# Chores tied behind evictions in the retention, another product order in the convolution, and a reordered passage from projection to gate/up

## The chip, the cores and the metric

One Trainium2 chip, one of its cores. The metric is the device time of one execution in microseconds (us), the median of three runs. The engines are named as in the profile: PE is TensorE, DVE is VectorE, ACT is ScalarE, POOL is GpSimd, SP is SyncE, which here only issues DMA. Each engine runs its own list of instructions in order; the lists are fixed when the program is built.

## The reference

```python
mod = silu(c) @ ada_w + ada_b                      # shift, scale, gate for both sub-layers
h = x * (1 + scale_m) + shift_m                    # x: 2048 rows of 1024
z = h @ w_in                                       # 3 x 512 columns: conv, 4 x 512: retention q, k, v, g
y_conv = bg * causal_conv3(cg * xin, conv_w)
q, k = rotary(q), rotary(k) * 128 ** -0.5          # 4 heads of 128, chunks of 128 rows
r = head_groupnorm(((q k^T) * decay_mask) v + decayed_state(q, k, v))
mix = concat(y_conv, silu(g) * r) @ w_out
x = layernorm(2 ** 0.25 * x + gate_m * mix)
h = x * (1 + scale_f) + shift_f
x = layernorm(2 ** 0.25 * x + gate_f * ((silu(h @ w_gate) * (h @ w_up)) @ w_down))
```

## The kernel before

All matrices are fp32 and are multiplied as pairs of fp16 numbers, a high and a low part: `mm3` issues three matmuls (high by high, L135; high by low, L136; low by high, L137) that add into one PSUM bank. The wide products after the retention go block by block with Strassen's and Winograd's scheme, in which seven products of blocks and of sums of blocks stand for eight. One such product is 12 matmuls of 128 rows by 512 columns for each quarter. PSUM has eight banks, four handed out in turn as `mm` (`bank`) and four as `ax` (`aux`); a bank is used again only after VectorE or ScalarE has read it ("eviction").

The program has these stages, which a scheduler merges: it takes the instructions in the order of the Python code, works out times for them with a model of its own, and writes each engine's list. `tc.issue_after(x)` adds the condition that what is issued under it comes after instruction `x` on the engine of `x`.

1. **Retention**, a loop over `t`, 16 tiles of 128 rows. `gemm_ret(t, u)` makes one of four 512-column groups of a tile (24 matmuls). Group `u == 0` is evicted by DVE (L705), `u` 1 and 2 by ACT (L709), `u == 3` by ACT with Silu (L711). `rotary(t)` (L734 to L736 on DVE, two sums on POOL) needs L709; `ret_scores` multiplies the scores by the decay mask on DVE (L767); `ret_y` (L793, L796 on PE) needs that product. Between the groups stand chores: `ret_h(p)` scales and shifts x by `modulate` (L296, eight instructions on ACT), makes the block sums on POOL, and `ret_hsplit(p)` splits them into fp16 pairs (L130 on ACT, L131 on DVE), which feed later tiles; `h_again` and `chores` do the same for tiles whose h planes go to DRAM (`hcscr`) for the convolution.
2. **Convolution**, `conv_pair(u, b)` for six column groups `u` and two row halves `b`. The products are numbered 0 to 6; `hp_load(b, m)` brings plane `m` of h from `hcscr`, `cw_split(u)` makes the weights (ACT L880 and L888, POOL sums, DVE L889).
3. **Output projection**, `op_half(t, half)`, evicted by DVE L1307 into the rows `y`; then `norm1` (statistics on DVE, L1278 on ACT), `y_store`, and `h2_pair(j)` with `h2_turn(j)`, which make and transpose the planes for the next stage (POOL L1342 to L1350, ACT L1351 and L1354, DVE L1341, L1352 and L1355, seven transposing DMAs L1374 on SP).
4. **Gate and up products**, `gu(q, bl)`, with weights from `gu_load`, `gu_scale`, `gu_split1` (planes A11, A12, S1, A22) and `gu_split2` (planes S2, S3, S4: L1421 to L1423, then ACT L1426 and DVE L1427).
5. **Down projection** and the second LayerNorm.

SP issues the loads in one list (`hcscr` and weight loads, transposes, stores of `y` and `u`), ACT issues the stores to `hcscr`.

## Time and profile before

| | us |
|---|---|
| median of three runs | 2106.2 |
| the three runs | 2104.92, 2106.2, 2108.79 |
| the profiled execution | 2106.87 |
| its span, first to last instruction | 2104.7 |

The span is 2.2 us shorter than the device time of the same execution. The mean clock granted to PE was 0.987 of full speed. Times below are counted from the span's start; line numbers are those of the kernel before.

### The profile page before, as it was taken

The page shows a single profiled execution, that of the slowest core. Times are in us where ns is not written, and L with a number is a line of the kernel's source. Part 1 is how long each engine was busy: PE and PEld are TensorE (multiplying, and loading weights), DVE is VectorE, ACT ScalarE, POOL GpSimd, SP SyncE. Part 2 cuts the span into 40 slices and gives each one's busy share as a digit, 9 for nine tenths or more (in the row PEclk, how much of TensorE's full clock was granted, in tenths as well). Part 3 has the DMA queues.
Part 4 walks back from the last instruction along what each step waited for, and adds up shares of the span by engine and source line. Part 5 has one row for each costly group of instructions (what it writes and reads, how often), then busy time and mean ns, then how long its engine had stood idle before and what let it go on. Part 6 is the DMA issues. An engine that isn't in the chain of part 4 may idle for free.

```text
span 2104.7 us, 24640 instructions
## 1 busy us (share of the span) xinstructions
PE 2023.1 (96%) x9631; PEld 948.0 (45%) x9631; DVE 1463.8 (70%) x1793; ACT 666.9 (32%) x728; POOL 904.9 (43%) x751
## 2 busy tenths in 40 slices
PE   8899998989899999789999999999999999999998
PEld 3354554444344544334444444444444444444443
DVE  7898846567686577766678768877777354478564
ACT  5523443433422223332323223343433222212210
POOL 3554855555642377742323114544444143134232
PEclk9999999999999999999999999999999999999999
DMA  9048544576873298742444553434343665375321
GB/s 380 26 135 260 163 133 110 161 236 212 269 307 125 85 251 195 186 128 71 149 170 166 184 189 126 160 126 154 131 150 120 237 263 198 139 272 190 150 77 74
DMA packets 189492, 361.06 MB, mean 172 GB/s; under 512 B 118080, under 2 KB 118080, under 8 KB 166592
## 3 DMA queue, kind: packets, MB, share of 16 engines
q1 hardware_dynamic: 181168, 344.55, 49.1%
q10 hardware_dynamic: 8208, 14.95, 2.1%
q8 instruction: 75, 1.23, 0.2%
q14 instruction: 41, 0.34, 0.0%
HBM read 231.26 MB, written 100.93 MB: 158 GB/s over the span
## 4 chain that ended last, share of the span: by engine, by line
PE 42%; DVE 8%; POOL 5%; DMA 5%; issue 2%; ACT 2%; SPq 0%; POOLq 0%; DVEq 0%; ACTq 0%
PE mm L135 7%; PE mm L136 7%; PE mm L137 7%; PE ax L135 7%; PE ax L137 7%; PE ax L136 7%; DMA pg<-yscr 2%; DMA pg<-in_w_dn_dram 2%; POOL pg L1342 1%; DVE pg L1617 1%; ACT pg L1278 1%; DVE wdm L87 1%; DVE pg L1618 1%; DVE pg L1482 1%; POOL rs L1270 1%
## 5 line engine op out<-in xcount | busy, mean ns | idle before, releaser
L135 PE MATMUL mm<-pg,pg 128*128 128x512 f16 x1604 | 609.4, 382 | 18.4 <-ACT pg L1426 8.2
L136 PE MATMUL mm<-pg,pg 128*128 128x512 f16 x1604 | 611.2, 381 | 0.0
L137 PE MATMUL mm<-pg,pg 128*128 128x512 f16 x1604 | 609.5, 381 | 1.7 <-DVE pg L889 1.7
L135 PE MATMUL ax<-pg,pg 128*128 128x512 f16 x1220 | 462.9, 380 | 9.3 <-DVE t2k L973 3.8
L137 PE MATMUL ax<-pg,pg 128*128 128x512 f16 x1220 | 462.6, 380 | 1.5 <-DVE pg L889 1.5
L136 PE MATMUL ax<-pg,pg 128*128 128x512 f16 x1220 | 463.3, 380 | 0.0
L136 PEld LDWEIGHTS <-pg 128*128 128x128 f16 x2888 | 283.3, 98 | 350.4 <-issue 23.7
L135 PEld LDWEIGHTS <-pg 128*128 128x128 f16 x2888 | 283.3, 98 | 345.7 <-issue 9.5
L137 PEld LDWEIGHTS <-pg 128*128 128x128 f16 x2888 | 283.1, 98 | 340.7 <-issue 6.4
L1476 POOL TENSOR_TENSOR pg<-pg,t2k 128x512 f32<-128x512 f32 x44 | 57.9, 1315 | 383.2 <-DVE t2k L1475 207.6
L131 DVE SCALAR_TENSOR_TENSOR pg<-pg,p2s,pg 128x2048 f16<-128x2048 f32 (+1 forms) x42 | 95.9, 2294 | 134.5 <-ACT pg L130 134.4
L130 ACT ACTIVATE pg<-pg,p2s 128x2048 f16<-128x2048 f32 (+1 forms) x42 | 77.6, 1858 | 262.2 <-PE mm L136 114.1
L87 DVE TENSOR_REDUCE m<-pg 128x2 bf16<-128x2048 f32 (+1 forms) x38 | 86.3, 2275 | 20.9 <-DMA pg<-in_w_gu_dram 10.8
L525 PE MATMUL mm<-pg,pg 128*128 128x512 f16 x384 | 89.1, 387 | 5.6 <-DVE pg L533 2.5
L1481 ACT ACTIVATE pg<-t2k,ivg 128x512 f32<-128x512 f32 x44 | 31.6, 717 | 178.1 <-DVE t2k L1480 178.1
L1530 DVE TENSOR_TENSOR pg<-pg,pg 128x2048 f16<-128x2048 f32 (+1 forms) x22 | 46.3, 2103 | 44.6 <-ACT pg L1529 44.6
L1413 DVE TENSOR_TENSOR pg<-pg,pg 128x2048 f16<-128x2048 f32 x22 | 51.7, 2349 | 31.7 <-ACT pg L1412 31.7
L1529 ACT ACTIVATE pg<-pg 128x2048 f16<-128x2048 f32 (+1 forms) x22 | 37.3, 1697 | 99.6 <-DMA wscr<-pg 57.8
L131 DVE SCALAR_TENSOR_TENSOR pg<-pg,hs,pg 128x1024 f16<-128x1024 f32 x32 | 49.4, 1547 | 26.8 <-ACT pg L130 26.6
L1270 POOL TENSOR_SCALAR rs<-mv 128x1 f32<-128x1 f32 x32 | 30.5, 957 | 82.2 <-DVE mv L1268 79.6
L1583 POOL TENSOR_TENSOR pg<-pg,pg 128x2048 f32<-128x2048 f32 (+1 forms) x6 | 26.9, 4491 | 82.0 <-DVE pg L131 38.6
L525 PEld LDWEIGHTS <-pg 128*128 128x128 f16 x384 | 37.5, 99 | 52.4 <-issue 7.7
(278 smaller groups left out, 2782.7 us busy)
## 6 DMA issues: line engine op xcount, KB each, us to landing
pg<-wscr SPq DMA_DIRECT2D x28, 1024.0 KB, 4.8
pg<-in_w_gu_dram SPq DMA_DIRECT2D x22, 1024.0 KB, 4.9
uscr<-pg SPq DMA_DIRECT2D x44, 512.0 KB, 2.8
pg<-in_w_dn_dram SPq DMA_DIRECT2D x22, 1024.0 KB, 5.9
pg<-in_adaT_dram SPq DMA_DIRECT2D x21, 1024.0 KB, 8.2
wscr<-pg SPq DMA_DIRECT2D x77, 256.0 KB, 2.9
yscr<-pg SPq DMA_DIRECT2D x16, 1024.0 KB, 4.3
pg<-uscr SPq DMA_DIRECT2D x16, 1024.0 KB, 5.7
```

What stands on the lines that cost most here:

```text
L87: return nc.vector.tensor_reduce(dst, src, axis=AX.X, op=OP.max, apply_absolute_value=True).ins
L130: nc.scalar.activation(hi, src, AF.Copy, scale=s)
L131: nc.vector.scalar_tensor_tensor(lo, src, s, hi, op0=OP.mult, op1=OP.subtract)
L135: nc.tensor.matmul(ps, l_hi, r_hi, start=start, stop=False, skip_group_check=again)
L136: nc.tensor.matmul(ps, l_hi, r_lo, start=False, stop=False, skip_group_check=again)
L137: return nc.tensor.matmul(ps, l_lo, r_hi, start=False, stop=stop, skip_group_check=again).ins
L525: nc.tensor.matmul(ps, hv[:, a, k, o], w[:, k], start=n == 0 and k == k0, stop=n == 2 and k == k1 - 1)
L1270: nc.gpsimd.tensor_scalar(rs, mv[:, 1:2], EPS / (ALPHA * ALPHA), None, op0=OP.add)
L1413: nc.vector.tensor_sub(wa[:, 2048:], pg, wa[:, :2048])
L1476: nc.gpsimd.tensor_add(e5, e5, p1)
L1529: nc.scalar.activation(o[:, :n, 0], src, AF.Copy)
L1530: nc.vector.tensor_sub(o[:, :n, 1], src, o[:, :n, 0])
```

## The change

- In the retention, `ret_h` and `ret_hsplit` come on ACT after the eviction of `gemm_ret(t, 2)`, and `h_again` and `chores` after that of `gemm_ret(t, 3)`. In the last tile the h planes 6 and 3 change places in the order of loading, and so does the list `ahead`.
- In `conv_pair` product 3, into a fresh bank, is issued before product 6, which adds into an old one.
- In the passage from stage 3 to stage 4 all of the last projections are issued before their LayerNorms; `gu_split2(0)` runs on VectorE, `gu_split2(1)` is done early; the scaling of the last two rows (`norm1`'s ACT instruction) comes after the products have begun; `h2_pair(3)` writes into the scratch page `s32[0]` and not in place; and `gu(0, 1)` and `gu(1, 1)` get `late=True`, by which the products with the planes S2, S4 and S3 come last.

```diff
+    evicted = [None]
...
-            nc.scalar.activation(dst, ps, AF.Copy, scale=iv)
+            evicted[0] = nc.scalar.activation(dst, ps, AF.Copy, scale=iv).ins
...
-            hp_load(0, 6)
+            hp_load(0, 3)
         if t % 2 == 0 and p < 8:
-            ret_h(p)
-            ret_hsplit(p)
+            with tc.issue_after(evicted[0]):
+                ret_h(p)
+                ret_hsplit(p)
...
+        with tc.issue_after(evicted[0]):
+            if t in AGAIN:
+                h_again(AGAIN.index(t))
+            elif chores:
+                chores.pop()()
...
         prod(pa, 1, False, True)
+        pd = new()
+        prod(pd, 3, True, True)
         prod(pb, 6, False, True)
         nc.vector.scalar_tensor_tensor(p1, pb, iv, p1, op0=OP.mult, op1=OP.add)
         nc.gpsimd.tensor_add(e5, e5, p1)
-        pd = new()
-        prod(pd, 3, True, True)
...
-        fp = yp[j] if tp else page()
+        fp = tp or page()
...
-        prod(pb, "S2", T2, True, True)
-        nc.vector.tensor_add(u2, pb, p1)
+        if not late:
+            prod(pb, "S2", T2, True, True)
+            nc.vector.tensor_add(u2, pb, p1)
...
+        if late:
+            prod(pb, "S2", T2, True, True)
+            nc.vector.tensor_add(u2, pb, p1)
+            prod(pc, "S4", B22, False, True)
+            nc.vector.tensor_add(u2, pc, u2)
         prod(pb, "S3", T3, False, True)
...
-            gu_split2(0, nc.gpsimd)
+            gu_split2(0, nc.vector)
+            for t in (2 * j, 2 * j + 1):
+                op_half(t, 1)
+            free(*wo_pages[2:])
+            for n in range(2):
+                gu_pages[n].append(page(F16, at=-1))
+            gu_split2(1, nc.vector)
...
-    gu_split1(1)
-    gu_split2(1, nc.vector)
+    gu(0, 1, late=True)
+    with tc.issue_after(gu_act[0]):
+        gu_split1(1)
+    with tc.issue_after(gu_act[1]):
+        for scaled in last_rows:
+            scaled()
+    y_store(3)
...
-    gu(1, 1)
+    gu(1, 1, late=True)
...
-    gu_scale(2)
+    with tc.issue_after(gu_pe[0]):
+        gu_scale(2)
```

Three places in the engines' lists. First ACT in the retention, at tile 10, in the kernel before: `mm282`, `mm283` and `mm287` are the banks of three groups of that tile, L296 the chore's scaling, L130 its splits, L356 its stores.

```order
L296 ACTIVATE pg16_91<-pg16_91,mod_103,msc_117 128x256 x8
L130 ACTIVATE pg22_97<-pg15_90,hs_139 128x2x512
L709 ACTIVATE pg12_87<-mm282_2743,iv4243_2222 128x512
L130 ACTIVATE t2k281_2738<-pg14_89,s280_2733 128x512
L356 DMA hcscr03_144<-pg22_97 128x1024
L709 ACTIVATE pg12_87<-mm283_2776,iv4243_2222 128x512
```

The same place in the changed kernel, where L709 is L710 and L711 is L712:

```order
L710 ACTIVATE pg12_87<-mm282_2743,iv4243_2222 128x512
L130 ACTIVATE pg16_91<-pg3_78,hs_139 128x2x512
L356 DMA hcscr06_147<-pg16_91 128x1024
L356 DMA hcscr04_145<-pg16_91 128x1024
L710 ACTIVATE pg12_87<-mm283_2776,iv4243_2222 128x512
L130 ACTIVATE pg16_91<-pg3_78,hs_139 128x2x512
L130 ACTIVATE t2k281_2738<-pg14_89,s280_2733 128x512
L356 DMA hcscr05_146<-pg16_91 128x1024
L356 DMA hcscr02_143<-pg16_91 128x1024
L712 ACTIVATE pg12_87<-mm287_2825,iv4243_2222 128x512
L296 ACTIVATE pg15_90<-pg15_90,mod_103,msc_117 128x256 x8
```

The eight scalings stood ahead of both evictions and now stand behind all three; the splits of the chore before, of page pg3, have come in between.

Second, DVE in the convolution's fifth unit, in the kernel before: `ax411` and `ax408` are banks of that unit, `g413` leads to the scale of the next unit's weights (`s412`), and L1157 works on the output projection's weights.

```order
L982 SCALAR_TENSOR_TENSOR t2k409_4221<-ax411_4288,ivc_110,t2k409_4221 128x512
L984 SCALAR_TENSOR_TENSOR t2k410_4222<-ax408_4220,ivc_110,t2k410_4222 128x512
L104 TENSOR_REDUCE g413_4324<-ax414_4325 128x1
L999 SCALAR_TENSOR_TENSOR pg10_85<-ax406_4218,ivc_110,t2k410_4222 128x4x128
L114 TENSOR_SCALAR e415_4328<-g413_4324 128x1
L116 TENSOR_SCALAR e415_4328<-e415_4328 128x1
L117 TENSOR_SCALAR s412_4323<-e415_4328 128x1
L1004 SCALAR_TENSOR_TENSOR pg6_81<-pg10_85,convw_101,pg6_81 128x1024
L1157 TENSOR_TENSOR pg23_98<-pg23_98,pg18_93 128x2048
```

And in the changed kernel, where L1157 is L1160, L973 is L974 and L1004 is L1005:

```order
L1160 TENSOR_TENSOR pg23_98<-pg23_98,pg18_93 128x2048
L104 TENSOR_REDUCE g413_4324<-ax414_4325 128x1
L983 SCALAR_TENSOR_TENSOR t2k409_4221<-ax411_4274,ivc_110,t2k409_4221 128x512
L87 TENSOR_REDUCE m450_4927<-pg23_98 128x1
L114 TENSOR_SCALAR e415_4328<-g413_4324 128x1
L974 SCALAR_TENSOR_TENSOR t2k420_4351<-mm417_4348,ivc_110,t2k419_4350 128x512
L116 TENSOR_SCALAR e415_4328<-e415_4328 128x1
L1005 SCALAR_TENSOR_TENSOR pg6_81<-pg10_85,convw_101,pg6_81 128x1024
L117 TENSOR_SCALAR s412_4323<-e415_4328 128x1
```

The instruction on the projection's weights and their absolute maximum (L87) now stand ahead of the four small ones that make `s412`.

Third, DVE at the passage, in the kernel before: `mm661`, `ax662` and `mm667` are banks of the last projections, L1352 and L1355 belong to `h2_pair(2)`, L1427 to `gu_split2(0)`.

```order
L1355 TENSOR_TENSOR pg16_91<-t2k645_6600,pg16_91 128x512
L1307 SCALAR_TENSOR_TENSOR pg4_79<-mm661_6702,io655_6635,pg4_79 128x512
L1267 BN_STATS st663_6730<-pg4_79 128x6
L1352 TENSOR_TENSOR pg17_92<-pg22_97,pg17_92 128x4x512
L1355 TENSOR_TENSOR pg16_91<-t2k646_6601,pg16_91 128x512
L1307 SCALAR_TENSOR_TENSOR pg4_79<-ax662_6716,io655_6635,pg4_79 128x512
L1427 TENSOR_TENSOR pg14_89<-pg21_96,pg14_89 128x1536
L1307 SCALAR_TENSOR_TENSOR pg4_79<-mm667_6741,io658_6666,pg4_79 128x512
```

And in the changed kernel, where L1307 is L1313, L1352 is L1358, L1355 is L1361, L1421 to L1423 are L1429 to L1431, L1427 is L1435, and `mm667` is `mm663`:

```order
L1430 TENSOR_TENSOR pg21_96<-pg9_84,pg21_96 128x512
L1431 TENSOR_TENSOR pg21_96<-pg9_84,pg21_96 128x512
L1361 TENSOR_TENSOR pg16_91<-t2k645_6600,pg16_91 128x512
L1313 SCALAR_TENSOR_TENSOR pg4_79<-mm661_6702,io655_6635,pg4_79 128x512
L1358 TENSOR_TENSOR pg17_92<-pg22_97,pg17_92 128x4x512
L1270 BN_STATS st665_6763<-pg4_79 128x6
L1435 TENSOR_TENSOR pg14_89<-pg21_96,pg14_89 128x1536
L1313 SCALAR_TENSOR_TENSOR pg4_79<-ax662_6716,io655_6635,pg4_79 128x512
L1361 TENSOR_TENSOR pg16_91<-t2k646_6601,pg16_91 128x512
L1361 TENSOR_TENSOR pg16_91<-t2k647_6602,pg16_91 128x512
L1313 SCALAR_TENSOR_TENSOR pg4_79<-mm663_6730,io658_6666,pg4_79 128x512
```

The sums of `gu_split2(0)` have come onto this list, L1435 has moved ahead of two evictions, and the eviction of the last `mm` bank stands behind all of `h2_pair(2)`. On PE, `gu(0, 1)` now begins with A11 (bank `mm673`), S1 (`mm675`), A22 (`mm678`, which takes over the bank of `mm663`) and A12, before S2 (`mm674`).

## Rows read from the trace of the kernel before

**Rows 1.** Windows by stage: length, busy time (instructions) of each engine, clock, DMA.

```profile
206.00:460.00 254.00, 237.04 (x1252) 126.18 (x1251) 164.99 (x292) 104.15 (x149) 148.16 (x132) 0.97 0.53 155
...
848.00:945.00 97.00, 80.45 (x357) 34.95 (x357) 70.77 (x87) 34.52 (x37) 53.83 (x49) 0.95 0.58 150
```

**Rows 2.** Waits of PE, 206 to 460: total us, times, longest.

```profile
PE ax L793 <- DVE pg L767: 12.1, 5, 4.3
PE ax L793 <- DVE g L125: 2.8, 1, 2.8
```

**Rows 3.** Windows of PE at half clock: length, busy (instructions), granted clock, DMA.

```profile
350.80:357.60 6.80, 4.60 (x19) 0.50 0.44 96
...
879.90:886.70 6.80, 3.90 (x10) 0.50 0.69 155
...
sum 30.60, PE 25.50; mean PE 3.64
```

**Rows 4.** Timeline of ACT, 338 to 349.5: start, duration, instruction, idle before.

```profile
340.75 4.04 ACT L296 ACTIVATE pg<-pg,mod,msc 128x256 f32<-128x256 f32 x8 [11.12 <-DMA pg<-in_xT_dram]
...
345.73 0.67 ACT L709 ACTIVATE pg<-mm,iv 128x512 f32<-128x512 f32 x1
```

**Rows 5.** Timeline of DVE, 336 to 354.

```profile
348.20 1.75 DVE L735 TENSOR_TENSOR pg<-pg,pg 128x512 f32<-128x512 f32 x1
...
352.21 0.74 DVE L767 SCALAR_TENSOR_TENSOR pg<-ax,pg,mask 128x512 f32<-128x512 f32 x1
```

**Rows 6.** Waits of PE, 460 to 600.

```profile
PE ax L135 <- DVE t2k L973: 3.8, 1, 3.8
PE ax L137 <- DVE pg L889: 1.5, 2, 1.2
PE mm L135 <- ACT t2k L971: 0.9, 1, 0.9
PE mm L135 <- DVE t2k L973: 0.9, 1, 0.9
```

**Rows 7.** Timeline of DVE, 544 to 566.

```profile
546.89 0.28 DVE L104 TENSOR_REDUCE g<-ax 128x1 f32<-128x128 f32 x1
...
552.33 3.10 DVE L1157 TENSOR_TENSOR pg<-pg,pg 128x2048 f32<-128x2048 f32 x1 [1.27 <-DMA pg<-in_w_out_dram]
...
557.22 2.27 DVE L87 TENSOR_REDUCE m<-pg 128x1 bf16<-128x2048 f32 x1
561.55 4.42 DVE L889 TENSOR_TENSOR pg<-pg,pg 128x2048 f16<-128x2048 f32 x2 [2.06 <-ACT pg L888]
```

**Rows 8.** Waits of PE, 848 to 945.

```profile
PE mm L135 <- ACT pg L1426: 8.2, 1, 8.2
PE mm L135 <- issue: 2.8, 1, 2.8
PE ax L135 <- ACT t2k L1463: 1.9, 1, 1.9
PE mm L135 <- DMA pg<-pg: 1.0, 1, 1.0
```

**Rows 9.** Timeline of POOL, 868 to 884.

```profile
872.57 1.26 POOL L1421 TENSOR_TENSOR pg<-pg 128x512 f32<-128x512 f32 x1
873.79 1.71 POOL L1348 TENSOR_TENSOR pg<-pg 128x512 f32<-128x512 f32 x1
```

**Rows 10.** Timeline of DVE, 864 to 935.

```profile
877.48 2.63 DVE L1352 TENSOR_TENSOR pg<-pg,pg 128x2048 f16<-128x2048 f32 x1 [1.71 <-ACT pg L1351]
...
882.77 1.76 DVE L1427 TENSOR_TENSOR pg<-pg,pg 128x1536 f16<-128x1536 f32 x1 [0.34 <-ACT pg L1426]
884.45 0.74 DVE L1307 SCALAR_TENSOR_TENSOR pg<-mm,io,pg 128x512 f32<-128x512 f32 x1
```

**Rows 11.** Timeline of DVE, 902 to 935.

```profile
903.04 4.64 DVE L1341 TENSOR_TENSOR pg<-pg,pg 128x512 f32<-128x512 f32 x4 [4.42 <-DMA yscr<-pg]
```

**Rows 12.** Timeline of SP, 912 to 930.

```profile
915.19 11.39 SPq L1374 DMA_TRANSPOSE pg<-pg  x7
```

More of the change, by code (lines that the diff above doesn't have):

```diff
@@ L708, in gemm_ret @@
         elif u != 3:
-            nc.scalar.activation(dst, ps, AF.Copy, scale=iv)
+            evicted[0] = nc.scalar.activation(dst, ps, AF.Copy, scale=iv).ins
         else:
-            nc.scalar.activation(dst, ps, AF.Silu, scale=iv)
+            evicted[0] = nc.scalar.activation(dst, ps, AF.Silu, scale=iv).ins
     qk_s, rot = {}, {}
@@ L1130 @@
             free(*ret_pages[6:8])
-            hp_load(0, 3)
+            hp_load(0, 6)
             hp_load(0, 2)
@@ L1134 @@
             ret_mix(2)
-        if t in AGAIN:
-            h_again(AGAIN.index(t))
-        elif chores:
-            chores.pop()()
+        with tc.issue_after(evicted[0]):
[3 more added lines that the diff above has]
+                chores.pop()()
         if t % 2 == 1:
@@ L1169, in wo_split @@
         free(*wo_stage.pop(g))
-    ahead = [0, 5, 4, 1, 6, 3, 2]
+    ahead = [0, 5, 4, 1, 3, 6, 2]
     for b in range(2):
@@ L1277, in norm1, with scaled @@
         nc.gpsimd.tensor_scalar(nm, mean, rs, -1.0, op0=OP.mult, op1=OP.mult)
-        nc.scalar.activation(y, y, AF.Identity, scale=rs, bias=nm)
+        def scaled():
+            nc.scalar.activation(y, y, AF.Identity, scale=rs, bias=nm)
+        return scaled
     def norm(y, lnp, pool_add):
@@ L1343, in h2_pair @@
         if tp:
-            t = [tp[:, i * 512:(i + 1) * 512] for i in range(3)]
+            t = [owner[id(hl[1])][1][:, 1536:2048], yp[j][:, :512], yp[j][:, 512:1024]]
         else:
@@ L1414, in gu_split1 @@
         av = wa.rearrange("p (a s k n) -> p a s k n", a=2, s=4, k=4)
-        gu_w[q] = {"A11": av[:, :, 0], "A12": av[:, :, 1], "S1": av[:, :, 2], "A22": av[:, :, 3], "pages": [wa]}
+        w = gu_w.setdefault(q, {"pages": []})
+        w.update({"A11": av[:, :, 0], "A12": av[:, :, 1], "S1": av[:, :, 2], "A22": av[:, :, 3]})
+        w["pages"].insert(0, wa)
     def gu_split2(q, eng):
-        pg = gu_stage.pop(q)
+        pg = gu_stage[q]
         a = pg.rearrange("p (s n) -> p s n", s=4)
@@ L1428, in gu_split2 @@
         bv = ws[:, :3072].rearrange("p (a s k n) -> p a s k n", a=2, s=3, k=4)
-        w = gu_w[q]
+        w = gu_w.setdefault(q, {"pages": []})
         w.update({"S2": bv[:, :, 0], "S3": bv[:, :, 1], "S4": bv[:, :, 2], "tmp": owner[id(ws)][1][:, 1536:2048]})
@@ L1436, in gu_done, with gu @@
         gu_pages[1].append(ws)
-    u32, ucount, gu_last, gu_pe = [], [0], [None], [None]
+    u32, ucount, gu_last, gu_pe, gu_act = [], [0], [None], [None], [None, None]
     uscr = [[dram.tile([2, P, NCH, 512], F32, name=f"uscr{b}{r}") for r in range(2)] for b in range(2)]
     um = const.tile([P, 2, NFF], F32, name="um")
-    def gu(q, bl, between=None):
+    def gu(q, bl, between=None, late=False):
         w = gu_w[q]
@@ L1462, in gu @@
         prod(pa, "A11", B11, True, True)
-        nc.scalar.activation(p1, pa, AF.Copy)
-        prod(pb, "S2", T2, True, True)
-        nc.vector.tensor_add(u2, pb, p1)
+        gu_act[0] = nc.scalar.activation(p1, pa, AF.Copy).ins
+        if not late:
+            prod(pb, "S2", T2, True, True)
+            nc.vector.tensor_add(u2, pb, p1)
         prod(pc, "S1", T1_, True, True)
@@ L1470, in gu @@
         prod(pa, "A12", B21, False, True)
-        nc.scalar.activation(u[:, 0], pa, AF.Silu, scale=iv_g)
+        gu_act[1] = nc.scalar.activation(u[:, 0], pa, AF.Silu, scale=iv_g).ins
         pd = new()
         prod(pd, "A22", T4, True, True)
+        if late:
[3 more added lines that the diff above has]
+            nc.vector.tensor_add(u2, pc, u2)
         prod(pb, "S3", T3, False, True)
@@ L1478, in gu @@
         nc.vector.scalar_tensor_tensor(u[:, 0], p1, iv_u, u[:, 0], op0=OP.mult, op1=OP.mult)
-        prod(pc, "S4", B22, False, True)
-        nc.vector.tensor_add(u2, pc, u2)
+        if not late:
+            prod(pc, "S4", B22, False, True)
+            nc.vector.tensor_add(u2, pc, u2)
         nc.scalar.activation(u[:, 1], u2, AF.Silu, scale=iv_g)
@@ L1656 @@
     order = (0, 1, 4, 5, 6, 7, 2, 3)
+    last_rows = []
     for i, j in enumerate(order):
@@ L1680 @@
                 op_half(t, 0)
-            op_half(t, 1)
-            norm1(ytile(t))
+                op_half(t, 1)
+            scaled = norm1(ytile(t))
+            if i < 7:
+                scaled()
+            else:
+                last_rows.append(scaled)
         if j % 2 == 1:
@@ L1690 @@
                 h2_turn(j)
-        else:
-            y_store(j)
         if i == 5:
             gu_load(1)
-    free(*wo_pages[2:])
-    for i in range(2):
-        gu_pages[i].append(page(F16, at=-1))
-    gu_split1(1)
-    gu_split2(1, nc.vector)
+    gu(0, 1, late=True)
[3 more added lines that the diff above has]
+        for scaled in last_rows:
+            scaled()
+    y_store(3)
     free(*gu_pages[2])
     gu_pages[2].clear()
-    gu(0, 1)
     for pl in (B11, T2, T1_, B21, T3, T4, B22):
@@ L1722 @@
     gu_max(3)
-    gu_scale(3)
+    with tc.issue_after(gu_pe[0]):
+        gu_scale(3)
     gu(1, 0)
```

## The prediction

> **What bounds it now.** I read the stages first. PE is the engine that the end waits for: over the passage (848 to 945) it is busy 80.45 of 97 us, over the retention (206 to 460) 237.04 of 254 [rows 1]. Next I read who ended PE's waits in those stages. In the retention it is one place in the loop, `ret_y` waiting for the masked scores: 12.1 us in five waits and 2.8 in one more that stands behind a chore's row on DVE [rows 2], 14.9 in all. In the convolution it is bank and weight waits, 3.8 for L973, up to 1.5 for L889, 0.9 each for L971 and L973 [rows 6], some 7 us. At the passage it is 8.2 for `gu_split2` (L1426), 2.8 and 1.0 at `gu(0, 0)`, 1.9 for L1463 [rows 8], 13.9 in all. Last I read the granted clock: seven stretches at its lower level (0.5, that is 1.2 of 2.4 GHz), 30.6 us together, each behind a wait of PE of over 2 us [rows 3]. A product takes twice its time there, so half of such a stretch is lost: four of them lie in the retention (17.0 us, 8.5 lost), one in the convolution (3.4, 1.7 lost), two in the passage (6.8 and 3.4, 5.1 lost). What the three edits can touch is therefore 14.9 + 8.5, 7 + 1.7 and 13.9 + 5.1, some 51 us; 2106.9 less that is the floor. The start-up before 206 us is not touched.
>
> **Retention.** The work is the same, only ACT's order differs. The longest wait shows the mechanism: eight scalings of a chore begin at 340.75, after 11.12 us in which ACT stood waiting for their x load, and two evictions of the tile stand behind them; the first runs at 345.73 [rows 4]. The rotary on DVE follows, then the mask product, which ends at 352.95 [rows 5], and PE has waited 4.3 [rows 2]. In the new order the evictions stand ahead of the load's wait and of 4.04 us of scalings, so the rotary can begin when its product is done. The place covers more than any of the six waits is long (4.3 at most), so all 14.9 and the clock's 8.5 could go: upper bound 23.4. Below, a chore that is moved back has to be paid somewhere. Each is eight scalings (4.04), four splits of 1.1 on ACT by the difference of its neighbours (345.73 less 340.75 and 4.04 leaves about 1 [rows 4]), the matching splits on DVE, block sums on POOL, and seven stores on ACT's queue. The splits of the older chore now stand between two evictions (first place in the lists), the page that they fill is freed later, and at the end of the retention the planes of the last chores reach `hcscr` later, from where SP loads what the convolution begins with. Nothing in the trace of before shows these waits. I price three of them, one in the middle of the loop (a page that waits for one chore's scalings, 2 to 4), one at the last tile and one at the first unit of the convolution (each about 2), together 6 of the 23.4. Value taken: **17 gained**; bounds 23 and 6 (all three at a whole chore of about 8 would eat 17 of 23).
>
> **Convolution.** Product 3 needs a fresh bank, product 6 an old one that DVE must have read. So the waits for L973, 3.8 and 0.9, have 2.6 us more slack. But the second place in the lists shows what the scheduler has made of it: on DVE the step on the projection's weights (L1157) now stands ahead of L104 and the scale of the next unit's weights. L1157 cannot begin before 552.33, when its load lands; L104 ran at 546.89 [rows 7]. Behind it now: 552.33 + 3.10 + 0.28 + 2.27 for L87, and some 3 us for the three sums and the small rows between, gives `s412` at about 561 in place of 548.3. From there to the fp16 weights it takes one scaling, two sums and one copy on ACT and POOL; before, that took 13.3 us (548.3 to L889 at 561.55 [rows 7]) with other work of both engines in between, which is now over by then. I take half, 6.5, an estimate, so L889 begins near 567.6. The four products that can run without these weights end at about 565, allowing for some 4 us that PE waits in them for L971, which two rows of ACT now precede, and L973. So PE waits there for 3 us more and then for the second half of the weights (1 to 2). Old waits 7 and clock 1.7; new ones 4 + 3 + 1.5 and a clock's share of 1 to 2. I take **1 lost**; bounds 7 gained (the load is early, or the old order is met) and 5 lost.
>
> **Passage.** By the rows of before PE has done A11 of `gu(0, 1)` at 874.6 and then waits 8.2. It now has S1, A22 and A12 to do before S2, 3 x 2.6 = 7.8 us of cover. But A22 takes over the bank of the last projection, and its eviction stands behind `h2_pair(2)` on DVE (third place in the lists). L1421's 1.26 is gone from POOL [rows 9], so L1352 may begin at 877.48 - 1.26 = 876.2; then L1352 2.63, the row statistics 0.7, L1427 1.76, an eviction 0.74, two sums of 0.7 and the eviction itself 0.74 [rows 10] (0.7 by the eviction's row, which has as many elements): 884.2. So PE does S1 until about 877.7 and waits again, 6.4 in place of 8.2, with the lower clock behind it as before. One product more is done when it goes on: 874.6 + 8.2 = 882.8 with one product, now 884.2 with two, a gain of 2.6 - 1.4 = 1.2. Then A12 of the next `gu` no longer follows at once on what ACT must read; the 1.9 for L1463 goes. Before `gu(0, 0)` stood a chain that began when `y`'s store had landed, since L1341 wrote in place: it waited 4.42 until 903.04 [rows 11], and seven transposes ran from 915.19 for 11.39 [rows 12]. Into the scratch page it need not wait for the store; it runs some 9 us earlier, and PE only some 6 earlier than before at that point. So 2.8 and 1.0 go, and 1.7 of the clock. Sum 1.2 + 1.9 + 3.8 + 1.7: **8.6 gained**. Bounds: 19 when A22's wait goes too, 2 when the load of the weights that DVE measures next (its L87 stands ahead of sums that `gu(0, 0)` waits for) takes the chain's gain.
>
> **A rule on the port.** In the trace, a DVE sum of two SBUF operands of 128x512 took 1.75 where another took 0.74 with one operand in PSUM [rows 5, 10]. The Trainium skill, page SBUF — State Buffer, section "SBUF: two separate sides", says that such an instruction and a GpSimd one lock a shared port pair, and one blocks for the other's whole instruction. By that the move of `gu_split2` from POOL to DVE buys less than the 1.26 suggests; it is the rival on DVE's price below, which is worked out from the rows alone.
>
> **Sum.** 17 - 1 + 8.6 = 24.6 off the profiled execution's 2106.9 (its span 2104.7 and 2.2 around it; 0.7 above the median of the runs) gives 2082.3; I say **2082**. A difference of about 0.2%, 4 us, is what a measurement of this kernel can tell from none.
>
> **Rivals.**
> - *Everything that waits goes*: 23 + 7 + 14 = 44, 2063. For it: all are waits for order, no engine but PE is over three quarters busy in these stages (DVE 164.99 of 254 and 70.77 of 97 [rows 1]). Against: the second and third places. Chance 0.13.
> - *The chores come back as waits* in the retention: gain 6 there, 6 - 1 + 8.6 = 14, 2093. For it: ACT's stores and pages are in a ring that the loop waits for. Chance 0.20.
> - *DVE is slower at the passage*: two sums and two of L1355 at 1.75 and not 0.7 put A22's wait 4.2 later, 8.6 - 4.2 = 4.4, 2086. Chance 0.12.
> - *The ties do nothing*: `rotary` could wait for something else as late as the eviction. Then 8.6 - 1 = 8, 2099. Against: the idle DVE ahead of it waits for ACT. Chance 0.05.
> - *Slower*: the last two chores (two times 4.04 of scalings, 4 of splits, sums and a store's landing, about 14) run after the last group, and the convolution's first planes come that much late: 28 lost against 24.6 gained, 2110. It decides when over 25 us of chores are left at the end. Chance 0.06.
>
> The forecast itself, 2074 to 2090, has 0.44. Range 2066 to 2099: it leaves out the slower case and half of the best one. Slower has 0.06, the slower case; same 0.04, the upper ends of "the ties do nothing" and "the chores come back"; faster 0.90.
>
> **What would show it.** Right: after 206 us no wait of L794 (old L793) over 2 us and no half clock there; a wait of about 6 us ahead of `mm678` for L1313; none ahead of the last transposes; in the convolution's fifth unit a wait of 3 us or more for the weights (L889 of the changed kernel). Wrong: waits of `gemm_ret` or of its rotary for a page; PE idle for over 5 us at the convolution's first products; A22 beginning at once behind S1.

## The result and the profile after

The changed kernel takes 2094.99 us (median of 4, 2092.37 to 2096.79) against 2106.53 for the kernel before; the ratio is 0.9943 with a 95% interval of 0.9926 to 0.9961. It is faster by 11.5 us; 24.6 were forecast. The profiled execution took 2094.44 (span 2092.7).

To see where, I follow four matmuls by their number in PE's list (902, 2159, 3941 and 4314; 2159 is the convolution's first product) and PE's last one. They start, or the last one ends, at 207.45, 461.55, 846.85, 947.77 and 2096.43 before, and at 206.06, 456.83, 843.28, 935.04 and 2083.91 after. The differences are the lengths of the retention loop, the convolution with most of the projections, the passage, and the rest:

| stretch (us) | before | after | gained | forecast |
|---|---|---|---|---|
| up to 902 | 207.45 | 206.06 | 1.4 | none |
| retention | 254.10 | 250.77 | 3.3 | 17 |
| convolution | 385.30 | 386.45 | -1.2 | -1 |
| passage | 100.92 | 91.76 | 9.2 | 8.6 |
| rest | 1148.66 | 1148.87 | -0.2 | none |

The first row is start-up, which the change doesn't touch; over all runs here it lies between 204.5 and 209.1. Two terms of the three came out; the retention did not. The windows of the changed kernel (length, busy time of PE, PEld, DVE, ACT, POOL, clock, DMA) answer to [rows 1]:

```profile
206.00:457.00 251.00, 234.57 (x1260) 126.17 (x1258) 159.65 (x291) 108.58 (x157) 148.30 (x133) 0.97 0.55 155
...
845.00:937.00 92.00, 81.56 (x378) 36.51 (x379) 71.94 (x88) 30.46 (x35) 47.92 (x42) 1.00 0.63 160
```

In the retention PE is still idle for 16.4 of 251 us, as it was for 17.0 of 254. But the idle time has other reasons. These are PE's waits from 206 to 458 (total us, times, longest), to be read against [rows 2]:

```profile
PE ax L135 <- DMA pg<-pg: 9.2, 3, 6.0
PE ax L99 <- DVE m L87: 4.5, 1, 4.5
PE ax L136 <- DMA pg<-pg: 1.8, 1, 1.8
PE ax L794 <- DVE pg L768: 0.9, 1, 0.9
```

The wait of `ret_y` for the mask product (L794, before L793) went from 14.9 to 0.9, as the change meant. In its place the scores (L135 into `ax`) wait for their transposed operands, which a DMA brings into a page, and the first weight of the convolution is late (L99). The lower clock, windows at half speed as in [rows 3], follows the new waits; the four lie in the retention (three, 13.6 us) and the convolution (one), none in the passage:

```profile
346.20:353.00 6.80, 5.52 (x26) 3.92 (x27) 4.51 (x5) 4.27 (x7) 4.44 (x3) 0.50 0.91 246
373.60:377.00 3.40, 3.15 (x16) 2.56 (x17) 1.99 (x5) 3.40 (x6) 1.87 (x3) 0.51 0.70 229
435.00:438.40 3.40, 3.40 (x15) 2.54 (x14) 3.40 (x3) 0.07 (x1) 0.22 (x1) 0.50 1.06 198
561.30:568.10 6.80, 5.43 (x13) 1.78 (x14) 5.41 (x4) 1.69 (x2) 5.87 (x4) 0.50 0.72 259
```

The longest wait, 5.95 us at 341.53, can be followed backwards. On PE the scores begin at 347.48, released by a DMA:

```profile
347.48 0.26 PE L135 MATMUL ax<-pg 128*128 128x128 f16 x1 [5.95 <-DMA pg<-pg]
```

SP issues those two transposes at 342.75:

```profile
342.75 3.66 SPq L754 DMA_TRANSPOSE pg<-pg  x2
```

That is when DVE has ended the second split of the chore of tile 10 (L131 at 341.44, 1.28 long; tiles count from 0). The transposes write into the page that this chore gives back; a run below that gives another page back first no longer has this wait:

```profile
330.39 1.26 DVE L131 SCALAR_TENSOR_TENSOR pg<-pg,hs,pg 128x1024 f16<-128x1024 f32 x1
...
341.44 1.28 DVE L131 SCALAR_TENSOR_TENSOR pg<-pg,hs,pg 128x1024 f16<-128x1024 f32 x1
```

Between the chore's two splits stand its four sums on POOL (L344 to L347), mixed with the small rows of `ret_y`:

```profile
331.73 1.27 POOL L344 TENSOR_TENSOR pg<-pg 128x512 f32<-128x512 f32 x1 [3.15 <-DVE pg L131]
332.96 0.20 POOL L805 TENSOR_TENSOR rs<-mv,pg 128x4 f32<-128x4 f32 x1
333.11 1.27 POOL L345 TENSOR_TENSOR pg<-pg 128x512 f32<-128x512 f32 x1
334.34 1.48 POOL L806 TENSOR_TENSOR rs<-rs,nhalf 128x4 f32<-128x4 f32 x1
335.80 2.21 POOL L346 TENSOR_TENSOR pg<-pg 128x512 f32<-128x512 f32 x1
337.97 1.03 POOL L808 TENSOR_TENSOR pg<-pg,rs 128x512 f32<-128x512 f32 x1
338.96 1.26 POOL L347 TENSOR_TENSOR pg<-pg 128x512 f32<-128x512 f32 x1
```

The wait of 4.54 for L99 ends in the same way. SP issues the load of the convolution's weight when a chore's second split has ended (425.57), and DVE can measure the weight (L87) when it has landed:

```profile
424.05 1.52 DVE L131 SCALAR_TENSOR_TENSOR pg<-pg,hs,pg 128x1024 f16<-128x1024 f32 x1
425.60 0.33 SPq L859 DMA_DIRECT2D pg<-in_w_conv_dram  x1
432.09 4.48 DVE L87 TENSOR_REDUCE m<-pg 128x1 bf16<-128x2048 f32 x2 [1.46 <-DMA pg<-in_w_conv_dram]
434.44 0.23 PE L99 MATMUL ax<-ident,m 128*128 128x128 f16 x1 [4.54 <-DVE m L87]
```

The chores themselves run much later than before. Their eight sets of scalings (L296 on ACT) began at 183, 206, 221, 265, 273, 293, 341 and 373, and now begin at 208, 245, 262, 314, 322, 344, 369 and 402: 25 to 51 us later. Before, they ran ahead of their place in the code; a tie holds each one back to it. The seventh set, at 340.75 in [rows 4], is now this one:

```profile
369.35 4.03 ACT L296 ACTIVATE pg<-pg,mod,msc 128x256 f32<-128x256 f32 x8
```

(In the first place of the lists, which is at tile 11, the scalings behind `mm287` are therefore not those that stood ahead of `mm282`, but the sixth set, at 344.25.)

So the reading of after gives three suspects: the chores that begin late, the page that they give back late, and POOL's sums in between. In the convolution (455 to 600) the old waits for L973 [rows 6] are gone and those for the weights have come:

```profile
PE ax L135 <- ACT pg L889: 3.7, 2, 2.6
...
PE mm L135 <- ACT t2k L972: 1.9, 1, 1.9
```

In the passage (845 to 940), against [rows 8]:

```profile
PE mm L135 <- ACT pg L1477: 2.9, 1, 2.9
PE mm L135 <- DVE pg L1313: 1.9, 1, 1.9
PE mm L135 <- DVE t2k L1486: 1.9, 1, 1.9
```

### The profile page after: what moved, and what is told of

Same layout as the page of the kernel before. It is cut to its first block, busy times and chain, and to the rows that moved or that the text cites. A ratio compares the mean times of both kernels' runs of the same rounds, so it can differ in the third digit from the quotient of the medians.

```text
span 2092.7 us, 24605 instructions
## 1 busy us (share of the span) xinstructions
PE 2015.8 (96%) x9631; PEld 945.4 (45%) x9631; DVE 1456.7 (70%) x1796; ACT 666.5 (32%) x728; POOL 906.0 (43%) x748
## 4 chain that ended last, share of the span: by engine, by line
PE 43%; DVE 9%; DMA 4%; POOL 4%; issue 2%; ACT 1%; SPq 0%; POOLq 0%; DVEq 0%; ACTq 0%
PE ax L135 7%; PE ax L136 7%; PE ax L137 7%; PE mm L135 7%; PE mm L137 7%; PE mm L136 7%; DMA pg<-in_w_dn_dram 2%; DMA pg<-yscr 2%; DVE wdm L87 1%; DVE pg L1498 1%; DVE pg L1435 1%; DVE pg L1633 1%; ACT pg L1283 1%; DVE pg L1634 1%; POOL pg L1348 1%
## 5 line engine op out<-in xcount | busy, mean ns | idle before, releaser
L135 PE MATMUL mm<-pg,pg 128*128 128x512 f16 x1604 | 606.8, 380 | 14.7 <-DVE t2k L1475 3.4
L135 PE MATMUL ax<-pg,pg 128*128 128x512 f16 x1220 | 463.7, 380 | 8.1 <-ACT pg L889 3.7
L135 PEld LDWEIGHTS <-pg 128*128 128x128 f16 x2888 | 283.3, 98 | 346.7 <-issue 12.4
L131 DVE SCALAR_TENSOR_TENSOR pg<-pg,p2s,pg 128x2048 f16<-128x2048 f32 (+1 forms) x42 | 92.7, 2216 | 137.9 <-ACT pg L130 137.8
L130 ACT ACTIVATE pg<-pg,p2s 128x2048 f16<-128x2048 f32 (+1 forms) x42 | 77.5, 1858 | 262.3 <-PE mm L136 114.1
L87 DVE TENSOR_REDUCE m<-pg 128x2 bf16<-128x2048 f32 (+1 forms) x38 | 86.2, 2276 | 14.3 <-DMA pg<-in_w_gu_dram 12.8
L131 DVE SCALAR_TENSOR_TENSOR pg<-pg,hs,pg 128x1024 f16<-128x1024 f32 x32 | 47.0, 1485 | 31.6 <-ACT pg L130 31.6
```

Of the source, the lines that this page charges most:

```text
L87: return nc.vector.tensor_reduce(dst, src, axis=AX.X, op=OP.max, apply_absolute_value=True).ins
L130: nc.scalar.activation(hi, src, AF.Copy, scale=s)
L131: nc.vector.scalar_tensor_tensor(lo, src, s, hi, op0=OP.mult, op1=OP.subtract)
L135: nc.tensor.matmul(ps, l_hi, r_hi, start=start, stop=False, skip_group_check=again)
```

## The experiments

Each ratio below is to the kernel before on the same chip, with its 95% interval. Lengths of stretches are worked out as in the table above, from one profiled execution of each kernel.

**The three parts alone.** The ties alone are the edits to the retention on the kernel before, with its order of the h planes kept:

```diff
         if t % 2 == 0 and p < 8:
-            ret_h(p)
-            ret_hsplit(p)
+            with tc.issue_after(evicted[0]):
+                ret_h(p)
+                ret_hsplit(p)
```

(and the same for `h_again` and `chores`).

> The kernel before with the ties of the retention alone. Theory A (in the retention the waits for the masked scores go, but the scores now wait for their transposes, whose target is a page that the tied chore gives back late; all of it belongs to the ties): the changed kernel began the convolution 4.7 us earlier, of which 0.4 lies in the start-up, so about 4 us faster than before, 2102 to 2103, with waits of over 2 us for DMA transposes and none over 1 us for L767 after 206 us. Rival B (the ties gain their 17 us, and another part of the change takes it away): 2088 to 2092 alone.

Measured 2105.11, 0.9982 [0.9971, 0.9993], about 4 us gained (1.5 to 6 by the interval). Its profiled execution, 2108.05, lies 2.9 above the median, and its retention takes 253.30, only 0.8 less than before. The waits are those of the changed kernel already: 9.2 for the transposes in three, 5.3 for L99, none for the mask product. So the missing gain is missing in the ties themselves.

The convolution's part alone moves product 3 ahead of product 6, and `hp_load` and `ahead` with it:

```diff
         prod(pa, 1, False, True)
+        pd = new()
+        prod(pd, 3, True, True)
         prod(pb, 6, False, True)
```

> The kernel before with the convolution's product order and its order of loads alone. Theory A: about 1 us slower (the changed kernel lost 1.1 us between the convolution's start and 848 us), 2107 to 2108, with a wait of 2 to 3 us for the weights in the fifth unit. Rival B (the loss came from the other parts' shift of the DMA times): 3 to 7 us faster, the old waits for L973 gone and no wait for the weights.

Measured 2108.78, 0.9994 [0.9985, 1.0003]: no change that can be told. Its convolution takes 385.70, before 385.30. The waits are those that the theory named: none for L973, and 2.6 and 1.1 for the weights.

The passage alone leaves both other parts out.

> The kernel before with the reordered passage alone. Theory A: 8 to 9 us faster, about 2098, with waits of 2 to 3 us in place of the 8.2, none of them followed by the lower clock. Rival (the passage gains only since the stages before it moved): 2103 or more.

Measured 2101.14, 0.9962 [0.9949, 0.9974], 8.0 us gained; its passage takes 91.96, with waits of 2.9, 1.9 and 1.9 in place of the 8.2 and no window at half clock. The three parts add up (4 + 1 + 8 = 13 by these ratios) to the 11.5 to 14 of the whole, so what they lose they don't lose to each other.

**Where the tie is put.** `h_again` and `chores` come behind the third group's eviction and not the fourth's, a group of 24 matmuls sooner.

```diff
+        second = evicted[0]
         gemm_ret(t, 3)
...
-        with tc.issue_after(evicted[0]):
+        with tc.issue_after(second):
```

> The changed kernel with h_again and the chores tied to the eviction of the tile's third group instead of its fourth. Theory A (the page is given back too late because the chore begins too late): the chore begins up to one group, 5.3 us, earlier, so the waits of 5.95 and 2.85 us for the transposes shrink by half or more and 3 to 10 us are gained over the changed kernel, 2085 to 2092. Rival C (the page comes late because of the chain of sums on POOL and splits, whenever the scalings run): within 2 us of the changed kernel, 2093 to 2097.

Measured 2101.42, 0.9963 [0.9950, 0.9975]: 4 to 6 us slower than the changed kernel, what neither theory said. PE waits there 6.3 for POOL's L808, 5.2 for L768 and 7.2 for scores. On POOL the rows of two chores' sums are mixed: the second of them begins its scalings 2 us sooner than in the changed kernel (320.0 against 322.2) and its last sum 4 us later (343.4 against 339.0). That a chore begun sooner ends sooner falls with it. It was the first sign that POOL's list has a part in the end of a chore.

**The changed kernel again, and the page.** First the changed kernel on the chip of the next three runs.

> The changed kernel once more, as the measure for the three beside it: 0.994 to 0.995 of the kernel before.

Measured 2094.74, 0.9933 [0.9921, 0.9946]. The page: `h_again` gives back its h page first, the source next, so that the transposes take the page that is free sooner.

```diff
-        free(pg, g)
+        free(*first, pg, g)
...
-        h_more(p, pg, h)
-        free(h)
+        h_more(p, pg, h, (h,))
```

> The changed kernel, but h_again hands back its three pages in another order: first the one that is read out early (h, stored after the first splits), then the source and the last result. So the transposes' target is a page that is free early, and the next tile's rows go to the source page. Theory A (the transposes wait for the source page, which the chore's last split gives back): the waits of 5.95 and 2.85 us and their lower clock go, 8 to 16 us faster than the changed kernel run beside it. Rival D (the chore's chain of sums and splits holds something else as late, so the wait only changes its place): within 3 us of the changed kernel, with waits of the same size for another instruction.

Measured 2094.01, 0.9932 [0.9919, 0.9944]: the median doesn't tell it from the changed kernel. The profile tells more. The convolution's first product starts 2.6 us sooner after matmul 902 (248.16 against 250.77), but PE came to it with 3.9 and 2.3 to wait for its weights, and a wait of 5.5 for transposes is back at a later chore:

```profile
PE ax L135 <- DMA pg<-pg: 5.9, 2, 5.5
PE mm L135 <- ACT pg L888: 3.9, 1, 3.9
```

Another page moves the wait, it doesn't take the reason away.

**Which tie.** Only `ret_h` and `ret_hsplit` are tied, `h_again` and `chores` are not.

> The changed kernel with the tie of ret_h and ret_hsplit alone; h_again and the other chores go where the scheduler puts them. Theory A (late h_again costs what the ties gain): the waits for transposes at tiles 7, 10, 11 and the wait of 4.5 us at the last tile go, and of the old waits for the mask product those at tiles 10 and 11 come back (4.3 and 2.8 us): 0 to 8 us faster than the changed kernel. Rival (the ties of h_again carry the gain): 5 us slower or more.

Measured 2097.03, 0.9943 [0.9930, 0.9957], within the intervals the same as the changed kernel. The waits lie elsewhere (8.3 at 424.00 for DVE's L123), their sum is about the same. Not conclusive on the ties.

**The step on the projection's weights.** `wo_max(0)` (L1160) is tied behind the last weight split of the convolution.

```diff
-                wo_max(0)
+                with tc.issue_after(cw_last[0]):
+                    wo_max(0)
```

> The changed kernel with the step on the output projection's first weights tied behind the last split of the convolution's weights on VectorE, so that the small instructions for those weights' scale come first again. Theory A (this step in front of them makes the waits of 2.6 and 1.1 us in the fifth unit, and their lower clock): those waits go and 4 to 7 us are gained over the changed kernel. Rival (the weights are late for another reason, or the tied step then stands in the way of an eviction): within 2 us of the changed kernel.

Measured 2094.38, 0.9931 [0.9918, 0.9943]. In the profile the waits of 2.6 and 1.1 for L889 are gone, and the convolution takes 383.60, 2.9 less than in the changed kernel: the forecast had the mechanism right. But the medians show none of it; its profile lost as much in the retention (254.15).

**The convolution's first weight.** On the kernel with the other page order the weight's scale comes ahead of `ret_y(13)` on DVE.

```diff
             cw_max(0)
+            with tc.issue_after(cw_scale(0)):
+                ret_y(t - 2)
```

> Edit: on top of the run that gives the chore's pages back in the order h, source, g (2094.01 beside a before of 2109.12, ratio 0.9932), the scale of the first conv weight is worked out ahead of ret_y(13) on VectorE instead of behind it. In that run PE had nothing to do from 449.91 to 453.78 and 454.38 to 456.70, both waits for the first conv weight's split, whose scale stood on VectorE behind four L810 that wait for POOL's L807. Theory A (this chain takes the page's gain back at the start of the convolution): the two waits (6.2) fall under 2 together, the convolution's first matmul comes 3 to 4 us sooner, ratio 0.991 to 0.9925. Rival (the split now holds up L810 and the last tiles' work on VectorE and POOL, and the wait moves to the last scores or into the first conv units): ratio 0.993 to 0.995.

Measured 2099.55, 0.9962 [0.9948, 0.9975], some 6 us slower than without it. The rival's case: the wait for the weight is gone and PE waits 7.0 for the last mask product, which now stands behind the weight's split:

```profile
PE ax L793 <- DVE pg L767: 7.0, 1, 7.0
```

**Edits together.** The other page order with the tied `wo_max(0)`:

> Edit: the page order h, source, g together with wo_max(0) tied behind the last conv weight's split on VectorE. Alone, the second took the waits of 2.64 and 1.10 us near 559 to 563 and shortened 543 to 600 from 57.0 to 54.1 us in its profile. Theory A (independent gains add): the 2.9 us are kept, ratio 0.9915 to 0.9925. Rival (each is taken back later, by the weights' chain or by the next wait): ratio 0.993 to 0.994, like either alone.

Measured 2093.52, 0.9926 [0.9914, 0.9938]: between the two expectations, not to be told from either alone. With the first weight's edit as well:

> Edit: all three: pages in the order h, source, g; the first conv weight's scale ahead of ret_y(13); wo_max(0) tied behind the last conv weight's split. Theory A: gains add to 6 to 7 us on the changed kernel, ratio 0.990 to 0.9915. Rival (what is won at one place is waited away at the next): ratio 0.992 to 0.994.

Measured 2098.30, 0.9948 [0.9935, 0.9961]: the rival or worse, for the reason of the run before it.

**The sums left out.** The chores leave out their four sums, first on the kernel with the other page order.

```diff
-        h_sums(pg)
         g, _ = h_split(pg, hs[:, 0:1])
```

> Edit: page order h, source, g, and the chores leave out the four sums on POOL (h_sums) ahead of the second split, so what the second split stores is not the sums: the output is not the reference's. Theory A (what is left of the retention's waits hangs on POOL's queue: in the run with the page order alone PE waited 5.50 us at 389.57 for transposes whose operands stood on POOL behind the chore's last sum): that wait and the 2.73 at 328.8 go, the stretch from 206 to the last retention matmul is 5 to 8 us shorter than the 243 us of that run; the convolution's start then waits longer for its weight, and the total falls by 1 to 4, ratio 0.9915 to 0.9930. Rival (the waits hang on the splits on VectorE and ScalarE): the waits stay within 1 us, ratio 0.993 to 0.994.

Measured 2081.16, 0.9870 [0.9857, 0.9883]: 13 us faster than with the sums. The theory expected 1 to 4, so it was right in what and wrong in how much; the rival is out. Its retention takes 235.72 in place of 248.16. Then on the changed kernel, pages as they were:

> Edit: the changed kernel with the four sums left out of the chores, and its pages given back as they were: what the second split stores is not the sums, so the output is not the reference's. Theory A (POOL's queue alone holds the retention): as fast as with the page order too, ratio 0.987 to 0.9885. Rival (the page given back last is a wait of its own, worth the 6 us that its order was worth in the stretch): ratio 0.990 to 0.992.

Measured 2075.86, 0.9846 [0.9832, 0.9859], 19 us faster than the changed kernel. The retention takes 230.10 in place of 250.77. These are the window and all of PE's waits from 206 to 440:

```profile
206.00:440.00 234.00, 229.42 (x1261) 122.83 (x1260) 156.13 (x298) 110.37 (x159) 101.20 (x104) 0.99 0.62 177
...
PE mm L137 <- DVE pg L889: 2.3, 1, 2.3
PE mm L135 <- ACT pg L888: 2.2, 1, 2.2
```

No wait of the loop is left; the two are the convolution's first weight. POOL is busy 101 and not 148 us. The page needs no edit: with the sums gone the old order of pages is no worse (0.9846 against 0.9870, whose intervals just touch). This kernel leaves work out, so its time is a bound and not a version to keep; and the sums were not left out of the kernel before, so it does not say what the ties are worth without them.

**The sums elsewhere.** All four on DVE, with the other page order:

```diff
-        nc.gpsimd.tensor_add(a22, a22, a21)
-        nc.gpsimd.tensor_sub(a21, a11, a21)
-        nc.gpsimd.tensor_sub(a11, a22, a11)
-        nc.gpsimd.tensor_sub(a12, a12, a11)
+        nc.vector.tensor_add(a22, a22, a21)
+        nc.vector.tensor_sub(a21, a11, a21)
+        nc.vector.tensor_sub(a11, a22, a11)
+        nc.vector.tensor_sub(a12, a12, a11)
```

> Edit: page order h, source, g, and the chores' four sums on VectorE in place of POOL; the output is the reference's. In the run with the page order alone POOL spends 43 us on the 32 sums of the 8 chores (10.6 + 11.0 + 10.2 + 11.1), and VectorE takes 0.68 us for an addition of the same shape (L735), 22 us for all. Theory A (POOL's queue holds the retention): the stretch from 206 to the convolution gets to between 231 us (sums left out) and 238; ratio 0.988 to 0.991. Rival (VectorE, busy 154 of 244 us there, becomes what is waited for): 241 us or more, ratio 0.993 to 0.997.

Measured 2087.55, 0.9897 [0.9884, 0.9911]; the retention takes 243.88, which is more than the theory's 238, though the time is in its range. The last two sums only:

> Edit: page order h, source, g, and the last two of the chores' four sums on VectorE. Theory A: half of POOL's relief, ratio 0.9895 to 0.992. Rival (VectorE is waited for, or the hand-over between the two engines costs what it saves): ratio 0.993 to 0.996.

Measured 2089.79, 0.9902 [0.9889, 0.9916], as good within the intervals. On the changed kernel, pages as they were:

> Edit: the changed kernel with the chores' four sums on VectorE, its pages given back as they were; the output is the reference's. Theory A (POOL's sums are the cause, the page order is no part of it, as without the sums the page order made no gain): ratio 0.988 to 0.9905, as with the page order (0.9897) or better. Rival (with the sums on VectorE the page is a wait again): 0.991 to 0.993.

Measured 2087.04, 0.9885 [0.9872, 0.9899]; the retention takes 237.57, 13.2 less than in the changed kernel, and the convolution 388.67, 2.2 more. With `wo_max(0)` tied as well:

> Edit: as before, with wo_max(0) tied behind the last conv weight's split as well. Theory A (the 2.9 us of the stretch 543 to 600 are kept, nothing later takes them): ratio 0.9865 to 0.9892. Rival (they are taken back): as without it, within 0.0007.

Measured 2082.84, 0.9865 [0.9850, 0.9880]: the fastest version that does all the work, 28 us under the kernel before and 12 (by the medians) to 16 (by the ratios) under the changed one. Its convolution takes 384.73, 3.9 less than in the run before it (388.67), and its retention 239.49, 1.9 more. By the medians the tie is worth 4.2, as forecast, but the two intervals overlap. Last, the kernel before, with nothing but the sums on DVE:

> Edit: the kernel before the change with the chores' four sums on VectorE: no ties, no conv order, no passage. Theory A (the ties' gain is capped by POOL: in the kernel before PE waits for evictions on ScalarE behind the chores' work, and POOL's relief alone gives little): ratio 0.998 to 1.000. Rival (the sums on POOL held the kernel before as well, and the relief alone gives most of what it gives the changed kernel, 7 us): 0.9955 to 0.9975.

Measured 2098.34, 0.9941 [0.9929, 0.9954]: 12.3 us, more than the rival said and three times what the ties are worth. The retention takes 240.95, 13.2 less than before, and the convolution 389.00, 3.7 more. PE's waits from 206 to 449 are these and two more of together 0.7:

```profile
PE ax L793 <- DVE pg L767: 8.0, 3, 4.3
PE ax L135 <- DMA pg<-pg: 0.7, 1, 0.7
```

and in the changed kernel with the sums on DVE (206 to 446):

```profile
PE ax L99 <- DVE m L87: 4.9, 1, 4.9
PE ax L135 <- DMA pg<-pg: 3.2, 2, 1.9
```

So the sums held the kernel before as well. With them on DVE the ties take the 8.0 for L767 away and bring 8.1 of others, and the step from 0.9941 to 0.9885 is 11.8 us, of which the passage has 8.0: the ties and the convolution are left with some 4 us, as with the sums on POOL. In the loop alone the sums' move is worth 13.2 without the ties and with them, and all the other edits 3.4 with the sums on DVE and 3.3 with them on POOL. (The convolution's part and the passage alone leave the loop at 254.1 and 254.0, so this is the ties; in their own run it was 0.8.) The two gains add; neither is the key to the other.

## Why the prediction came out as it did

**Retention, 17 forecast, 3.3 in the profile, 4 by the ties alone: the step that failed.** It is the price of the new waits, "together 6 of the 23.4". What the ties were to take away, they took: `ret_y`'s wait fell from 14.9 to 0.9. But the new waits are 9.2 and 1.8 for transposes into a page and 4.5 for the convolution's first weight. The lower clock costs half of the time that PE is busy in its windows, 14.8 us before and 12.1 after. So the loop lost 17.0 + 7.4 = 24.4 us before and 16.4 + 6.0 = 22.4 after: these rows hold 2.0 of the 3.3, where 17 were forecast.

Two slips of the sum hid this. Half of a whole window at half clock was taken as lost, 8.5, though in one of them PE was busy for only 4.60 of 6.80 [rows 3] and the rest is the wait itself, counted already: 7.4. And three new waits of a whole chore of 8 are 24 and not 17, so the lower bound was no gain at all, and not 6.

I had the kinds of wait right (a page in the middle, the last tile) and took them for side effects of some rows that change places. What the ties did is hold every chore back by 25 to 51 us, and the two longest new waits, 5.95 and 4.54, both end when such a chore's second split gives its page back. The others (2.85 and 1.8) were not followed back. I had followed ACT's idle time to the x load [rows 4] and no further: that load, issued at 335.79, had waited for a page too, until a chore's store (L356) had landed at 335.71.

How long a chore takes from its scalings to that page was not in the forecast either, and there POOL comes in. It was on the page before the change: POOL is busy 148.16 of 254 us [rows 1], and its eight chores' sums took 52 of these (L344 12.0, L345 14.7, L346 11.8, L347 13.5, by the groups of before), each 1.27 at best and up to 2.2. I read POOL as an engine with room. Without the sums the loop has none of these waits (230.10, 20.7 less); with them on DVE it is 13.2 shorter, on either kernel. So the sums on POOL are shown to hold the loop. They are not shown to be what kept the ties at 3 to 4 us: with the sums on DVE the ties exchange one wait for another just the same. Nor do these runs tell apart POOL's load and the length of the chore, since the move changes both. The best loop that does all the work takes 237.57, 16.5 less than before: 13.2 by the place of the sums, 3.4 by the ties.

**The rivals.** "The chores come back as waits" (6 gained, 2093) came nearest to 2095. "The ties do nothing" is out by the ties alone; "slower" had its mechanism, the last chore that runs late, but at 4.5 us (L99) and not 28.

**Convolution, 1 lost, 1.2 measured.** The step (L1157 ahead of the next weights' scale, so PE waits "3 us more and then for the second half") is seen: 2.6 and 1.1 for L889, 1.9 for L972, and tying L1160 later takes 2.9 off. By the profiles PE waits 9.7 up to 600 us before and 9.2 after, and loses 1.7 and 2.7 by the lower clock. That the part alone measures nothing fits.

**Passage, 8.6 gained, 9.2 measured, 8.0 alone.** The sum came out, but not by its items. A22 was to wait 6.4 for the bank of the last projection. It did not wait, which the forecast had named as a sign of being wrong. These rows of the changed kernel show it:

```profile
876.58 0.38 PE L135 MATMUL mm<-pg,pg 128*128 128x512 f16 x1 [0.74 <-ACT t2k L1472]
877.40 1.73 DVE L1435 TENSOR_TENSOR pg<-pg,pg 128x1536 f16<-128x1536 f32 x1
880.92 0.73 DVE L1313 SCALAR_TENSOR_TENSOR pg<-mm,io,pg 128x512 f32<-128x512 f32 x1
881.71 0.38 PE L135 MATMUL mm<-pg,pg 128*128 128x512 f16 x1 [1.95 <-DVE pg L1313]
```

PE runs three products from 868.34 on without a wait. The fourth, at 876.58, waits for ACT's copy of A11 (L1472): it is A12, the only one that adds into A11's bank. The fifth, at 881.71, waits for the eviction. It is S2: its plane is ready when L1435 has ended, at 879.13, too late for the first three, which are therefore A11, S1 and A22. So by these rows it is S2 that takes over the bank of `mm663`, and not A22, as was said ahead of the prediction. The eviction's own time was priced well: it ended at 881.65, where 884.2 less the 3.6 by which all of it is earlier is 880.6. Only, PE had done A22 and A12 by then.

So S2 begins 2.5 us later than before (by the same shift) with three products of 2.6 done ahead of it, 5.3 gained. Two new waits then take 4.8 of this back: 2.9 for L1477, ACT's copy of S1, which stands on ACT behind the split L1434 and so behind `gu_split2(1)` on DVE, and 1.9 for L1486. No lower clock follows them, 2.0 gained. In place of the forecast's 1.2 these make 2.5. The chain to `gu(0, 0)` did as said: 2.8, 1.0 and 1.9 are gone, 0.8 is left. With the 1.7 of its lower clock that is 2.5 + 3.0 + 1.9 + 1.7 = 9.1. That 8.6 came so near is in part luck: what A22 did not wait, two other waits cost.

**The rule on the port.** The sums of `gu_split2` on DVE in the changed kernel, beside POOL's sums, and a second time when POOL stood idle (874.72 to 885.51):

```profile
868.30 1.71 POOL L1353 TENSOR_TENSOR t2k<-pg 128x512 f32<-128x512 f32 x1
867.80 1.09 DVE L1430 TENSOR_TENSOR pg<-pg,pg 128x512 f32<-128x512 f32 x1
868.82 1.75 DVE L1431 TENSOR_TENSOR pg<-pg,pg 128x512 f32<-128x512 f32 x1
...
884.03 0.67 DVE L1430 TENSOR_TENSOR pg<-pg,pg 128x512 f32<-128x512 f32 x1
884.63 0.68 DVE L1431 TENSOR_TENSOR pg<-pg,pg 128x512 f32<-128x512 f32 x1
```

L1431 began behind POOL's L1353 and ended 0.56 after it (870.57 against 870.01). The spread of 0.67 to 1.75 agrees with the section cited in the prediction (the Trainium skill, SBUF — State Buffer, "SBUF: two separate sides"). The rival built on it, 4.2 us later, did not come: the two rows of L1361 ahead of the eviction (879.72) took 1.27 together, and the sums ran ahead of L1358.

**What stays open.** With the sums on DVE the retention takes 237.57, without them 230.10. DVE is busier by some 23 us there (179.31 against 156.13) and L99's wait of 4.9 stays; which of its rows holds that wait was not tried. The ties still hold the chores back in that kernel (the last one's scalings begin at 389.5, and at 363.9 without the ties), and no run kept the chores early and the evictions first. The order of the pages with the sums on DVE moves time between two stretches (243.88 and 383.69 with it, 237.57 and 388.67 without): together they differ by 1.3 us in one profile each.

## What to carry to other kernels

A tie that lets one instruction go first holds back everything that is tied behind it, here by 25 to 51 us, and what the held work hands on, here pages, comes later too. So list when each piece of the tied work runs before the change, not only what stands next to the tie. Before pricing a reorder, follow the wait to its last link (load, page, who gives the page back), and add up what that work costs on each engine, the one that looks half idle too. An experiment that leaves the suspected work out sizes it at once, where single moves of waits gave nothing that could be measured, or a loss.

## What the runs showed of the hardware

By the times of one place, a small instruction on POOL was held for as long as DVE ran several instructions one behind the other. In the run with the other page order, POOL's L804, 128x4 elements, took 3.49 us where its sister in the changed kernel took 0.20:

```profile
380.35 3.49 POOL L804 TENSOR_TENSOR rs<-mv,pg 128x4 f32<-128x4 f32 x1 [1.36 <-DVE mv L802]
```

DVE ran four instructions with two SBUF operands without a gap in that time, and POOL's ended (383.84) when the last of these did (383.79):

```profile
380.19 1.25 DVE L131 SCALAR_TENSOR_TENSOR pg<-pg,hs,pg 128x1024 f16<-128x1024 f32 x1
381.36 1.22 DVE L734 TENSOR_TENSOR pg<-pg,pg 128x1024 f32<-128x1024 f32 x1
382.50 0.68 DVE L735 TENSOR_TENSOR pg<-pg,pg 128x512 f32<-128x512 f32 x1
383.10 0.69 DVE L736 TENSOR_TENSOR pg<-pg,pg 128x512 f32<-128x512 f32 x1
```

So a POOL step in a chain can cost more beside a busy DVE than its own row elsewhere. The Trainium skill, Perfetto Trace Analysis, section "Optimizing Scalar/DVE Operations", warns that moving work between these two engines might not help, since they share a port. Here it did: in the changed kernel the chores' sums take 0.68 to 0.90 us on DVE in the mean and 1.32 to 1.73 on POOL, and the move was worth 12.3 us on the kernel before.

The lower clock did not cost anything in one place. In the second execution of the changed kernel a window of 3.4 us at half clock lies at 889.2 in the passage, where the first has none; the passage takes 91.94 in it and 91.76 in the first, and the wait of 1.9 for L1486 is not there: the slower products, which cost half of 3.4, filled it.
